# Hybrid Mamba-2 / latent-attention step: one mask tile, constant rows filled beside their tiles, an earlier table load; in the page stage a negated running maximum, two gather buffers and rotary keys read where they land

## The chip, the cores and the metric

The kernel runs on one core of a Trainium2 chip. The core has a matrix engine (TensorE, PE in the profile; its weight loads are listed as PEld), a vector engine (VectorE, DVE), an activation engine (ScalarE, ACT), a general engine (GpSimd, POOL) and a queue engine (SyncE, SP) that issues most DMA transfers. The metric is the device time of one launch in microseconds. The median of three runs of the kernel before is 1981.43 us (1976.2 to 1981.67).

## The reference, cut to what matters

Two layers work on a prompt (1 x 1024 tokens) and on a group of samples (8 sequences of 8 tokens, each with 2048 cached positions). Layer 0 is a Mamba-2 mixer, layer 1 is multi-head latent attention (MLA) with 16 heads; a norm follows. The change touches the attention of layer 1 only. All values are fp32.

```python
def latent_partial(q_lat, q_pe, ckv, kpe, mask):
    s = (jnp.einsum('bqhc,bkc->bhqk', q_lat, ckv)          # latent part, 256 wide
         + jnp.einsum('bqhr,bkr->bhqk', q_pe, kpe)) * MLA_SCALE   # rotary part, 32 wide
    if mask is not None:
        s = jnp.where(mask, s, NEG_INF)
    m = jnp.max(s, axis=-1)
    p = jnp.exp(s - m[..., None])
    return m, jnp.sum(p, axis=-1), jnp.einsum('bhqk,bkc->bhqc', p, ckv)

def merge_partial(pa, pb):
    m = jnp.maximum(ma, mb)
    ca, cb = jnp.exp(ma - m), jnp.exp(mb - m)
    return m, la * ca + lb * cb, aa * ca[..., None] + ab * cb[..., None]
# prompt: o = softmax(q k^T) v per head, causal, 1024 queries
# samples: latent_partial over the 8 new tokens, then one page of 128 positions after the other
#          (16 pages of the cache per sequence, picked by page_table), merged as above
# both: h = h + (o * silu(gate)) @ w_out ; y = rms_norm(h) * final_norm_w
```

## The kernel before, in words

Every fp32 product is made of three matmuls on rounded halves: a value x is split into `xh` (a cast to the matmul's rounded type fp32r) and `xl = x - xh`, and the product is `xh*wh + xl*wh + xh*wl`. ACT mostly makes the high halves, DVE or POOL the low ones.

The Mamba layer runs to about 1090 us, the projections of the MLA layer to about 1343 us. What the change touches comes after that.

**Prompt heads (`mla_heads`, about 1343 to 1712 us).** For each of 16 heads there are 12 blocks of 128 keys by up to 512 queries. `qk` makes scores `st` from `kTh/kTl` and `qTh/qTl`, ACT makes the exponential twice, once as a rounded high half `th` (L1341) and once as `P` (L1342), POOL or DVE the low half `tl = P - th` (L1344), and `pv` adds `th*Vh + th*Vl + tl*Vh` into `o` (L1361 to L1363). The tiles `qT` and `kT` have 98 rows: 96 of query or key and two constant rows (ones in `kTh`, zeros in `kTl` and `qTl`), which carry the negative row maximum into the matmul. The value tiles `V` have 64 columns of ones, which give the row sums. Between the blocks the program puts units of preparation: `maxpass` of the next head (`sc`, a reduction `mx` with the mask `mk`), `prep_kv` (keys `kp`, split into `kTh`, `kTl`), `prep_q` (`qs`, queries). Before the first block the tables of ACT are changed (a table load, L1390), and `Heads.open` fills the constant rows of four key tiles, of `qTl2` and of `V1` and loads the mask a second time, into a tile of its own.

**Pages of the sample group (`Sample.flow`).** 32 items, four for each sequence; an item is 512 cached positions. For one item: POOL gathers the rows `pgr` from the cache with an indirect DMA, ACT makes the high half `kvh` (L1632), POOL the low half `kvl` (L1633, one operation 1024 wide), PE transposes `pgr` into `ct` (L1622), ACT and DVE make `cTh`, `cTl`; seven matmuls make the scores `sc` (six latent ones and one with the rotary keys `tk`, which SP loads as `tkr` for two items and POOL rounds into `tk` for one, L1550). `softmax` then takes the maximum `mx` (L1567), the new running maximum `mn` (L1570), its negated scaled form `nm` (L1573), and ACT the exponential `P` (L1576) and the factor `f` for the old sums (L1580). PE transposes `P` into `pt` (L1660), ACT and DVE split it, and matmuls add to the output `o`; `ac` is the accumulator of a sequence. The first 11 steps of this flow lie between the blocks of heads 14 and 15; the others run with the output projection.

**Output projection (`MlaOut.pieces`).** Eight tiles of 128 prompt tokens: the heads' gated output `og` is loaded (0.5 MB), split into `oh` (ACT) and `ol` (DVE), multiplied with the halves `w5h`, `w5l` of the output weights (48 matmuls of 512 columns each for every half), added to the residual `h`, squared and summed (`sq`, `ss`), normed (L1877, `h<-h,ss,fw`) and stored. Its pieces are put between the items, one tile for every four items. The halves of the weights are made from `w5r`/`w5p` (L1808, L1809) when the heads have ended.

**What sets the order.** PE and POOL run in the order of the program, which is written by hand here (`step`, `turn`, `flow`, `merge`). ACT, DVE and the queue of SP are ordered by a scheduler with a model of the time of each operation, except for operations that the program pins with `keep_in_program_order`. Buffers come from pools; `bufs=1` means that a new tile of that tag waits until the last reader of the old one has ended. The tag `og5` is such a tag: the loaded `og` and the scratch tile `junk` of the squares share one buffer.

Of the kernel before, what the change touches and what calls it, by code (L numbers as in the profile page):

```python
# [16 lines left out]
D = 1024  # L17
# [51 lines left out]


def RT(nc):
    return nc.gpsimd.tensor_copy
# [1031 lines left out]
class Heads:  # L1104
    def __init__(self, k, st):
# [3 lines left out]
        self.wuv = I["mla_w_uv"][0].rearrange("c h n -> c (h n)")  # L1109
        vp = st.enter_context(open_pool(tc, name="vp3", bufs=1))  # L1110
# [3 lines left out]
        self.kT = [k.kT]  # L1114
        self.add_k(vp, 1)
        self.qT = []
# [3 lines left out]
    def start(self, st):  # L1120
        k, nc = self.k, self.k.nc
        self.sp = st.enter_context(open_pool(k.tc, name="q0", bufs=1))
        self.load_mask()
# [4 lines left out]
    def load_mask(self):  # L1128
        nc = self.k.nc
        mk = self.sp.tile([128, 640], F32, name="mk")  # L1130
# [31 lines left out]
    def open(self, st, psum):  # L1162
# [5 lines left out]
        for a, b in self.kT:  # L1168
            nc.gpsimd.memset(a[96:98].bitcast(F32), 1.0)
            nc.gpsimd.memset(b[96:98].bitcast(F32), 0.0)  # L1170
        self.add_q(sp, 2)
        self.add_v(sp, 1)
        self.load_mask()
# [12 lines left out]
    def prep_group(self, hg):  # L1186
# [10 lines left out]
        split(k, *wv, raw)  # L1197
        yield
# [18 lines left out]
    def prep_kv(self, h):  # L1217
# [171 lines left out]
def mla_heads(k, hd, sm, early, st):  # L1389
    k.tc.keep_in_program_order(k.nc.scalar.preload_act_table_set("natural_log_exp_and_others"))  # L1390
# [84 lines left out]
class Sample:  # L1475
# [65 lines left out]
    def load_tk(self, n):  # L1541
        k, nc = self.k, self.k.nc
        self.tkr = self.ep.tile([96, 4, 256], F32, tag="tkr", name=f"tkr{n}", bufs=1)
        for j in range(3):
            src = k.kpe_d[j % 2][:, :, 128 * n : 128 * n + 256].rearrange("r c x -> c r x")
            nc.sync.dma_start(self.tkr[32 * j : 32 * j + 32], src)

    def round_tk(self, n):
        tk = self.ep.tile([96, 4, 128], F32R, tag="tk", name=f"tk{n}", bufs=2)
        RT(self.k.nc)(tk, self.tkr[:, :, 128 * (n % 2) : 128 * (n % 2) + 128])  # L1550
        self.tk[n] = tk
# [12 lines left out]
    def softmax(self, name, s, n, m_old):  # L1564
# [3 lines left out]
        if m_old is not None:  # L1568
            m = self.small(name, "mn4", 1)
            nc.vector.tensor_scalar(m, mx, m_old, None, op0=ALU.max)  # L1570
            mx = m
        nm = self.small(name, "nm4", 1)
# [413 lines left out]
```

## Time and profile before

| | |
|---|---|
| median of the runs (three) | 1981.43 us (1976.2 to 1981.67) |
| the profiled execution: its time, its span | 1988.45 us, 1986.7 us |
| PE busy | 1909.0 us (96% of the span), 12001 matmuls |
| DVE, ACT, POOL busy | 1204.0 us (61%), 1110.3 us (56%), 837.9 us (42%) |
| mean granted TensorE clock | 0.988 of full speed |
| moved by DMA | 202.12 MB, mean 102 GB/s |

The span is the time from the first to the last instruction of the profiled execution. "Busy" leaves out register, branch and DMA-issuing instructions. In rows of groups the columns are the line, the engine, the operation, output and inputs with their shapes, the count, then the busy time, the mean of one in ns, and the idle time before the group with the work that ended it. In rows of the timeline they are start (us), duration (us), engine, line, operation, output and inputs, and in brackets the idle time of the engine just before, with what ended it.

### The profile page before, as it was taken

How to read it: one execution, taken by the hardware profiler on the slowest of the kernel's cores; microseconds unless marked ns; L12 is line 12 of the kernel's file. 1: busy time of each engine (PE TensorE's matmuls, PEld its weight loads, DVE VectorE, ACT ScalarE, POOL GpSimd, SP SyncE). 2: the span in 40 equal slices, each digit the busy share in tenths (PEclk: the TensorE clock that was granted, in tenths of full speed). 3: DMA queues.
4: the chain of work that ended last, by engine and by line, in shares of the span. 5: the costliest groups of instructions: out<-in, count | busy, mean ns of one | idle time of the engine just before them, and what ended most of it. 6: DMA issues, size and time to landing. Idle time of an engine off the chain costs nothing. (4 is left out here: it accounts for less than half of the span.)

```text
span 1986.7 us, 33396 instructions
## 1 busy us (share of the span) xinstructions
PE 1909.0 (96%) x12001; PEld 1738.7 (88%) x12001; DVE 1204.0 (61%) x2439; ACT 1110.3 (56%) x2535; POOL 837.9 (42%) x1018
## 2 busy tenths in 40 slices
PE   6999999999999999899999999998999999899998
PEld 5999999999999999788787998997888887688887
DVE  4557575756665656755434114566788787766665
ACT  5456666666666666633214224436777777645552
POOL 1537455555655555443003221204333335755541
PEclk9999999999999999999999999999999999899999
DMA  4223323332333332645433242222111113544441
GB/s 152 59 65 88 90 84 96 83 106 83 95 83 95 81 96 89 200 153 183 148 126 121 89 165 66 99 84 74 45 50 40 50 40 100 189 139 140 138 146 38
DMA packets 181228, 202.12 MB, mean 102 GB/s; under 512 B 18844, under 2 KB 147752, under 8 KB 180680
## 3 DMA queue, kind: packets, MB, share of 16 engines
q1 hardware_dynamic: 176008, 180.21, 29.9%
q0 software_dynamic: 4976, 19.66, 3.1%
q8 instruction: 95, 1.56, 0.3%
q14 instruction: 69, 0.57, 0.1%
q10 hardware_dynamic: 80, 0.13, 0.0%
HBM read 146.65 MB, written 53.28 MB: 101 GB/s over the span
## 5 line engine op out<-in xcount | busy, mean ns | idle before, releaser
L88 PE MATMUL pj<-xh,wih 128*128 128x384 f32 (+1 forms) x768 | 255.8, 337 | 5.0 <-ACT xh L250 4.4
L88 PE MATMUL pj<-xl,wih 128*128 128x384 f32 (+1 forms) x768 | 255.3, 332 | 0.6 <-DVE xl L251 0.6
L88 PE MATMUL pj<-xh,wil 128*128 128x384 f32 (+1 forms) x768 | 254.6, 332 | 0.0
L1344 POOL TENSOR_TENSOR tl<-P,th 128x384 fp32r<-128x384 f32 (+1 forms) x96 | 91.9, 957 | 160.8 <-ACT P L1342 119.2
L487 DVE SCALAR_TENSOR_TENSOR acc<-raw,vec,acc 128x1112 f32<-128x1112 f32 x96 | 141.6, 1476 | 25.8 <-ACT acc L483 24.9
L88 PEld LDWEIGHTS pj<-xh,wih 128*128 128x128 f32 x768 | 145.1, 190 | 6.8 <-ACT xh L250 5.1
L88 PEld LDWEIGHTS pj<-xl,wih 128*128 128x128 f32 x768 | 145.7, 190 | 1.9 <-DVE xl L251 0.9
L88 PEld LDWEIGHTS pj<-xh,wil 128*128 128x128 f32 x768 | 145.5, 189 | 0.4
L100 PE MATMUL pz<-wih,xh 128*128 128x256 f32 x504 | 142.8, 287 | 0.8 <-ACT z L528 0.8
L100 PE MATMUL pz<-wil,xh 128*128 128x256 f32 (+1 forms) x504 | 140.2, 284 | 0.0
L1341 ACT ACTIVATE th<-st 128x512 fp32r<-128x512 f32 x192 | 94.5, 492 | 75.7 <-PE st L1337 54.9
L591 ACT ACTIVATE M<-M,tok 128x128 f32<-128x128 f32 (+1 forms) x288 | 90.9, 386 | 68.6 <-DVE M L588 68.4
L100 PE MATMUL pz<-wih,xl 128*128 128x256 f32 x448 | 128.3, 286 | 0.0
L1633 POOL TENSOR_TENSOR kvl<-pgr,kvh 128x1024 fp32r<-128x1024 f32 x32 | 77.6, 2424 | 71.6 <-ACT kvh L1632 71.6
L100 PEld LDWEIGHTS pz<-wih,xh 128*128 128x128 f32 x504 | 96.0, 190 | 1.6 <-ACT z L528 1.2
L588 DVE TENSOR_TENSOR M<-M,negu 128x512 f32<-128x512 f32 x64 | 52.2, 815 | 69.0 <-DMA M<-acs_d 68.7
L1342 ACT ACTIVATE P<-st 128x512 f32<-128x512 f32 x192 | 93.4, 486 | 0.0
L100 PEld LDWEIGHTS pz<-wil,xh 128*128 128x128 f32 (+1 forms) x504 | 92.7, 184 | 0.7
L130 DVE TENSOR_TENSOR wil<-wraw,wih 128x512 fp32r<-128x512 f32 x88 | 71.2, 815 | 30.4 <-ACT wih L129 27.1
L1344 DVE TENSOR_TENSOR tl<-P,th 128x512 fp32r<-128x512 f32 x96 | 74.8, 779 | 21.8 <-ACT P L1342 21.3
L574 POOL TENSOR_TENSOR xdd<-xsT,tok 128x256 f32<-128x256 f32 x64 | 51.2, 800 | 81.3 <-ACT xsT L560 81.0
L100 PEld LDWEIGHTS pz<-wih,xl 128*128 128x128 f32 x448 | 85.3, 190 | 0.1
(827 smaller groups left out, 6343.5 us busy)
## 6 DMA issues: line engine op xcount, KB each, us to landing
wraw<-in_ssd_w_in SPq DMA_DIRECT2D x92, 256.0 KB
M<-acs_d SPq DMA_DIRECT2D x64, 256.0 KB
s<-in_state_ssm SPq DMA_DIRECT2D x32, 256.0 KB
y_d<-y SPq DMA_DIRECT2D x64, 128.0 KB
out_s_ssm<-s SPq DMA_DIRECT2D x32, 256.0 KB
wraw<-in_ssd_w_out SPq DMA_DIRECT2D x12, 512.0 KB
q_d<-qt SPq DMA_DIRECT2D x32, 192.0 KB
qp<-q_d SPq DMA_DIRECT2D x8, 768.0 KB
```

The costliest lines, as they stand in the source:

```text
L88: nc.tensor.matmul(out, a, b, start=(i == 0), stop=(i == n - 1))
L100: nc.tensor.matmul(o, a, b, start=(j == 0), stop=(j == len(ops) - 1))
L130: (eng or nc.vector).tensor_tensor(lo, src, hi.bitcast(F32), op=ALU.subtract)
L487: last = nc.vector.scalar_tensor_tensor(acc, raw[:, j : j + n], k.convw[j][:, blk : blk + 1], acc, op0=ALU.mult, op1=ALU.add)
L574: nc.gpsimd.tensor_tensor(v3(xdd), v3(xsT), hb(2), op=ALU.mult)
L588: nc.vector.tensor_tensor(M[:m, :, :m], M[:m, :, :m], (k.negs if smp else k.negu)[:m, :m].unsqueeze(1).to_broadcast([m, 4, m]), op=ALU.add)
L591: nc.scalar.activation(M[:m, h, :m], M[:m, h, :m], AF.Exp, bias=tk[:, 0, 4 * g + h : 4 * g + h + 1])
L1341: nc.scalar.activation(th[:, :n], ps[:, :n], AF.Exp, scale=SCALE)
L1342: nc.scalar.activation(P[:, :n], ps[:, :n], AF.Exp, scale=SCALE)
L1344: eng.tensor_tensor(tl[:, :n], P[:, :n], th[:, :n].bitcast(F32), op=ALU.subtract)
L1633: nc.gpsimd.tensor_tensor(rl, raw, rh.bitcast(F32), op=ALU.subtract)
```

## The change

1. The mask is loaded once, into a tile of the pool `qp` that lasts for the layer. The second load and its memset of 384 columns (L1131) are gone.
2. The constant rows of a key tile are filled when the tile gets its content (`ones_rows`): those of tiles 0 and 1 in `__init__`, those of 2 and 3 behind their rotary casts in `prep_kv`. The constant rows of `qTl2` are filled in `prep_q` of head 2, the ones columns of `V1` in `prep_group` of the second group of heads.
3. The table load of ACT stands in the loop of the query projection, 3 of its copies before the end, where it stood at the start of the heads.
4. `softmax` keeps `nm`, the negated and scaled running maximum, as its state: one operation takes the place of `mn` and `nm`, and `f` is the exponential of `nm - old`.
5. The rotary keys land in a tile of the rounded type and are read from there, the half of an item with a stride (4 runs of 128 columns, 256 apart); the round casts on POOL (32) are gone. All seven score matmuls now name their operands in three dimensions.
6. In `halves`, the cast `kvh` is kept in program order, and `kvl` is made by two operations of 512 columns.
7. `og5` has two buffers, and `junk` a tag of its own (`sq5`).

```diff
@@ Heads
+        self.load_mask()
         vp = st.enter_context(open_pool(tc, name="vp3", bufs=1))
...
         self.kT = [k.kT]
+        self.ones_rows(0)
         self.add_k(vp, 1)
+        self.ones_rows(1)
...
     def load_mask(self):
         nc = self.k.nc
-        mk = self.sp.tile([128, 640], F32, name="mk")
+        mk = self.k.qp.tile([128, 640], F32, name="mk")
...
     def add_q(self, pool, j):
-        self.k.nc.gpsimd.memset(t[1][96:98].bitcast(F32), 0.0)
+        if j < 2:
+            self.k.nc.gpsimd.memset(t[1][96:98].bitcast(F32), 0.0)
...
     def add_v(self, pool, j):
-        nc.gpsimd.memset(t[0][:, :, :, 64:128].bitcast(F32), 1.0)
-        nc.gpsimd.memset(t[1][:, :, :, 64:128].bitcast(F32), 0.0)
         self.V.append(t)
+        if j == 0:
+            self.ones_cols(0)
+
+    def ones_cols(self, j):
+        for t, x in zip(self.V[j], (1.0, 0.0)):
+            self.k.nc.gpsimd.memset(t[:, :, :, 64:128].bitcast(F32), x)
...
@@ Heads.open
-        for a, b in self.kT:
-            nc.gpsimd.memset(a[96:98].bitcast(F32), 1.0)
-            nc.gpsimd.memset(b[96:98].bitcast(F32), 0.0)
         self.add_q(sp, 2)
         self.add_v(sp, 1)
-        self.load_mask()
+
+    def ones_rows(self, j):
+        nc, (a, b) = self.k.nc, self.kT[j]
+        nc.gpsimd.memset(a[96:98].bitcast(F32), 1.0)
+        nc.gpsimd.memset(b[96:98].bitcast(F32), 0.0)
...
@@ Heads.prep_group
         split(k, *wv, raw)
+        if hg == 1:
+            self.ones_cols(1)
@@ Heads.prep_kv
             if pr == 1:
-                self.rope_keys(2)
-                self.rope_keys(3)
+                for x in (2, 3):
+                    self.rope_keys(x)
+                    self.ones_rows(x)
@@ Heads.prep_q
+        if h == 2:
+            nc.gpsimd.memset(self.qT[2][1][96:98].bitcast(F32), 0.0)
@@ mla_heads
-    k.tc.keep_in_program_order(k.nc.scalar.preload_act_table_set("natural_log_exp_and_others"))
@@ Sample.load_tk
-        self.tkr = self.ep.tile([96, 4, 256], F32, tag="tkr", name=f"tkr{n}", bufs=1)
+        tk = self.ep.tile([96, 4, 256], F32R, tag="tk", name=f"tk{n}", bufs=2)
         for j in range(3):
             src = k.kpe_d[j % 2][:, :, 128 * n : 128 * n + 256].rearrange("r c x -> c r x")
-            nc.sync.dma_start(self.tkr[32 * j : 32 * j + 32], src)
-
-    def round_tk(self, n):
-        tk = self.ep.tile([96, 4, 128], F32R, tag="tk", name=f"tk{n}", bufs=2)
-        RT(self.k.nc)(tk, self.tkr[:, :, 128 * (n % 2) : 128 * (n % 2) + 128])
-        self.tk[n] = tk
+            nc.sync.dma_start(tk[32 * j : 32 * j + 32].bitcast(F32), src)
+        for j in range(2):
+            self.tk[n + j] = tk[:, :, 128 * j : 128 * j + 128]
@@ Sample.softmax
-    def softmax(self, name, s, n, m_old):
+    def softmax(self, name, s, n, old):
         nc.vector.reduce_max(mx, s, axis=AX.X)
-        if m_old is not None:
-            m = self.small(name, "mn4", 1)
-            nc.vector.tensor_scalar(m, mx, m_old, None, op0=ALU.max)
-            mx = m
-        nm = self.small(name, "nm4", 1)
-        nc.vector.tensor_scalar(nm, mx, -SCALE, None, op0=ALU.mult)
+        nm = self.small(name, "nm4", 1, 4)
+        if old is None:
+            nc.vector.tensor_scalar(nm, mx, -SCALE, None, op0=ALU.mult)
+        else:
+            nc.vector.tensor_scalar(nm, mx, -SCALE, old, op0=ALU.mult, op1=ALU.min)
...
-            nc.scalar.activation(f, m_old, AF.Exp, bias=nm, scale=SCALE)
-        return mx, P, l, f
+            nc.scalar.activation(f, old, AF.Exp, bias=nm, scale=-1.0)
+        return nm, P, l, f
@@ Sample.halves
-        nc.scalar.copy(rh, raw)
-        nc.gpsimd.tensor_tensor(rl, raw, rh.bitcast(F32), op=ALU.subtract)
+        k.tc.keep_in_program_order(nc.scalar.copy(rh, raw))
+        for j in (0, 2):
+            nc.gpsimd.tensor_tensor(rl[:, j : j + 2], raw[:, j : j + 2], rh[:, j : j + 2].bitcast(F32), op=ALU.subtract)
@@ MlaOut.pieces
-                g = sp.tile([128, 8, 128], F32, tag="og5", name=f"og5{i}", bufs=1)
+                g = sp.tile([128, 8, 128], F32, tag="og5", name=f"og5{i}", bufs=2)
...
-            junk = sp.tile([128, D], F32, tag="og5", name=f"sq5{i}", bufs=1)[:m]
+            junk = sp.tile([128, D], F32, tag="sq5", name=f"sq5{i}", bufs=1)[:m]
@@ mla_q's loop
         for n, _ in enumerate(mla_q(k, mid)):
+            if n == 32:
+                tc.keep_in_program_order(nc.scalar.preload_act_table_set("natural_log_exp_and_others"))
```

The order of PE's instructions is the same in both kernels; the other engines' orders move at three places.

POOL where the heads begin, before: the memsets of the constant rows and columns and of the mask, then the first low half `tl` (384 wide), then the four rotary casts (`kTh`, `kTl` of key tiles 2 and 3) and the next low half.

```order
L1170 MEMSET kTl_15386 2x1024
L1137 MEMSET qTl_15396 2x1024
L1146 MEMSET Vh_15398 128x16x64
L1147 MEMSET Vl_15399 128x16x64
L1131 MEMSET mk 128x384
L1344 TENSOR_TENSOR tl<-P,th 128x384
L1160 CAST kTh_15383<-kTh_13121 32x1024
L1160 CAST kTl_15384<-kTl_13122 32x1024
L1160 CAST kTh_15385<-kTh_13121 32x1024
L1160 CAST kTl_15386<-kTl_13122 32x1024
```

The same place after: the first `tl` comes first, and the memsets of key tiles 2 and 3 stand among the casts.

```order
L1354 TENSOR_TENSOR tl<-P,th 128x384
L1163 CAST kTh_15388<-kTh_13121 32x1024
L1163 CAST kTl_15389<-kTl_13122 32x1024
L1176 MEMSET kTh_15388 2x1024
L1177 MEMSET kTl_15389 2x1024
L1163 CAST kTh_15390<-kTh_13121 32x1024
L1163 CAST kTl_15391<-kTl_13122 32x1024
L1176 MEMSET kTh_15390 2x1024
L1177 MEMSET kTl_15391 2x1024
L1354 TENSOR_TENSOR tl<-P,th 128x128
```

The memsets of `qTl2`, `V1` and the mask have left this place, and those of key tiles 2 and 3 have moved behind the first `tl`, ahead of the second.

ACT in the blocks of head 14, before: the exponentials `th`, `P` of the blocks and among them the casts `kvh` of the first two items.

```order
L1342 ACTIVATE P<-st_1_2_19755 128x512
L1374 ACTIVATE rl_0_19749<-rl_0_19749 64x512
L1632 CAST kvh<-pgr_19697 128x1024
L1341 ACTIVATE th<-st_1_3_19777 128x512
L1342 ACTIVATE P<-st_1_3_19777 128x512
L1632 CAST kvh<-pgr_19705 128x1024
L1341 ACTIVATE th<-st_1_4_19797 128x512
L1342 ACTIVATE P<-st_1_4_19797 128x512
L1341 ACTIVATE th<-st_1_5_19817 128x384
L1342 ACTIVATE P<-st_1_5_19817 128x384
```

The same place after:

```order
L1352 ACTIVATE P<-st_1_2_19752 128x512
L1384 ACTIVATE rl_0_19746<-rl_0_19746 64x512
L1351 ACTIVATE th<-st_1_3_19774 128x512
L1352 ACTIVATE P<-st_1_3_19774 128x512
L1351 ACTIVATE th<-st_1_4_19794 128x512
L1352 ACTIVATE P<-st_1_4_19794 128x512
```

And where the first `kvh` stands now, 18 operations further on, behind the exponential `P40n` of the first sequence's own tokens, between the first four and the last eight blocks of head 15:

```order
L1351 ACTIVATE th<-st_0_3_19957 128x128
L1352 ACTIVATE P<-st_0_3_19957 128x128
L1581 ACTIVATE P40n,l40n<-sn_19976,nm40n 128x8
L1637 CAST kvh<-pgr_19694 128x1024
L1351 ACTIVATE th<-st_1_0_19991 128x512
L1352 ACTIVATE P<-st_1_0_19991 128x512
```

The casts of the first two items have moved behind the blocks that they stood among.

DVE once in four items, where a tile of the output projection ends (`h`, `ss`) and the next one's `ol` is made, before:

```order
L1851 TENSOR_TENSOR h_21333<-h_21333,p_21523 128x512
L1681 SCALAR_TENSOR_TENSOR ac_21356<-ac_21356,f_21511,o_21647 128x256
L1868 TENSOR_TENSOR ss_21339<-ss_21339 128x1
L1869 TENSOR_SCALAR ss_21339<-ss_21339 128x1
L1877 SCALAR_TENSOR_TENSOR h_21333<-h_21333,ss_21339,fw 128x512 x2
L130 TENSOR_TENSOR cTl_0_21671<-ct_0_21665,cTh_0_21670 128x512
L130 TENSOR_TENSOR pTl_21680<-pt_21674,pTh_21679 128x512
L130 TENSOR_TENSOR cTl_1_21689<-ct_1_21683,cTh_1_21688 128x512
L1567 TENSOR_REDUCE mx_21700<-sc_21692 128x1
L130 TENSOR_TENSOR ol_21728<-og_21729,oh_21727 128x1024
L1570 TENSOR_SCALAR mn_21702<-mx_21700,mx44n 128x1
L1573 TENSOR_SCALAR nm_21704<-mn_21702 128x1
```

The same place after:

```order
L1855 TENSOR_TENSOR h_21289<-h_21289,p_21473 128x512
L126 TENSOR_TENSOR ol_21672<-og_21673,oh_21671 128x1024
L1687 SCALAR_TENSOR_TENSOR ac_21312<-ac_21312,f_21463,o_21594 128x256
L1872 TENSOR_TENSOR ss_21295<-ss_21295 128x1
L1873 TENSOR_SCALAR ss_21295<-ss_21295 128x1
L126 TENSOR_TENSOR cTl_0_21619<-ct_0_21613,cTh_0_21618 128x512
L1881 SCALAR_TENSOR_TENSOR h_21289<-h_21289,ss_21295,fw 128x512 x2
L126 TENSOR_TENSOR pTl_21628<-pt_21622,pTh_21627 128x512
L126 TENSOR_TENSOR cTl_1_21637<-ct_1_21631,cTh_1_21636 128x512
L1573 TENSOR_REDUCE mx_21648<-sc_21640 128x1
L1578 TENSOR_SCALAR nm_21650<-mx_21648,nm44n 128x1
```

The low half `ol` of the next tile has moved from between the reduction `mx` and `nm` to the start of the piece, `cTl` ahead of the norm of `h`, and `mn` is gone.

More of the change, by code (lines that the diff above doesn't have):

```diff
@@ L68 @@
 FLOW = 11
-def RT(nc):
-    return nc.gpsimd.tensor_copy
 def WQ(nc):
@@ L1577, in softmax @@
         f = None
-        if m_old is not None:
+        if old is not None:
             f = self.small(name, "f4", 1)
-            nc.scalar.activation(f, m_old, AF.Exp, bias=nm, scale=SCALE)
-        return mx, P, l, f
+            nc.scalar.activation(f, old, AF.Exp, bias=nm, scale=-1.0)
+        return nm, P, l, f
     def first_scores(self, b):
@@ L1628, in halves @@
     def halves(self, n):
-        nc, sp = self.k.nc, self.sp
+        k, nc = self.k, self.k.nc
         raw = self.raw.pop(n)
         rh, rl = (x[:, n % 2].rearrange("p (r c) -> p r c", r=4) for x in (self.k.kvh, self.k.kvl))
-        nc.scalar.copy(rh, raw)
-        nc.gpsimd.tensor_tensor(rl, raw, rh.bitcast(F32), op=ALU.subtract)
+        k.tc.keep_in_program_order(nc.scalar.copy(rh, raw))
+        for j in (0, 2):
+            nc.gpsimd.tensor_tensor(rl[:, j : j + 2], raw[:, j : j + 2], rh[:, j : j + 2].bitcast(F32), op=ALU.subtract)
         self.hl[n] = (rh, rl)
@@ L1640, in scores @@
         c0, c1 = self.cT.pop((n, 0)), self.cT.pop((n, 1))
-        mm3(nc, ps, [
+        mm3(nc, ps.rearrange("p (r c) -> p r c", r=4), [(x, y if len(y.shape) == 3 else y.rearrange("p (r c) -> p r c", r=4)) for x, y in (
             (k.qlh[:, 0, b], c0[0]), (k.qlh[:, 0, b], c0[1]), (k.qll[:, 0, b], c0[0]),
             (k.qlh[:, 1, b], c1[0]), (k.qlh[:, 1, b], c1[1]), (k.qll[:, 1, b], c1[0]),
-            (k.qpr[:, b], self.tk.pop(n))])
+            (k.qpr[:, b], self.tk.pop(n)))])
         self.ps[n] = ps
@@ L1737, in flow @@
                 self.late_loads()
-            if t:
-                self.round_tk(n + 1)
             if n % 2 == 0 and n + 2 < N:
@@ L1897, in layer_mla @@
         mla_in(k, right, mid)
-        qp = st.enter_context(open_pool(tc, name="qp", bufs=1))
+        k.qp = qp = st.enter_context(open_pool(tc, name="qp", bufs=1))
         k.qlh = qp.tile([128, 2, NB, 128], F32R, name="qlh")
```

1 line of the change is left out of this document (removed).

## The prediction

> **What bounds the kernel now.** I read the page's first part first, then PE's waits in the three stretches that the change touches, then a table of windows for the clock. The first line shares out the busy time.
>
> ```profile
> PE 1909.0 (96%) x12001; PEld 1738.7 (88%) x12001; DVE 1204.0 (61%) x2439; ACT 1110.3 (56%) x2535; POOL 837.9 (42%) x1018
> ```
>
> PE is the bound; no other engine is near full over the span. The change leaves PE's instructions and their order alone, so a gain can come only from PE's idle time and from time at a lowered clock. PE's waits in 1340 to 1366 us (where the heads begin), 1660 to 1746 (end of the heads and hand-over to the output projection) and 1762 to 1937 (steady pages) are, with total, count and longest in us:
>
> ```profile
> PE sc L1298 <- DVE mx L1303: 2.7, 2, 1.4
> PE o L1363 <- POOL tl L1344: 2.1, 1, 2.1
> ...
> PE act L1691 <- DVE ac L1684: 4.4, 1, 4.4
> PE pt L1660 <- ACT P L1576: 2.9, 3, 1.4
> PE o L88 <- DVE pTl L130: 2.0, 1, 2.0
> PE st L1330 <- ACT P L1342: 1.6, 1, 1.6
> PE o40n L1612 <- ACT pn L1605: 1.2, 1, 1.2
> ...
> PE pt L1660 <- ACT P L1576: 7.8, 6, 1.3
> ```
>
> That is 4.8, 12.1 and 7.8 us. Windows of the same execution, with window, length, busy time of PE, PEld, DVE, ACT, POOL, then PE's clock, DMA share and GB/s:
>
> ```profile
> 1359.00:1366.00 7.00, 6.42 (x19) 5.17 (x20) 3.21 (x8) 3.94 (x8) 3.13 (x4) 0.52 0.17 41
> 1672.00:1680.00 8.00, 7.13 (x25) 6.46 (x26) 2.31 (x7) 3.69 (x10) 3.37 (x4) 0.57 0.09 10
> 1680.00:1690.00 10.00, 10.00 (x68) 8.93 (x66) 7.09 (x9) 9.04 (x22) 6.99 (x7) 1.00 0.38 125
> 1693.00:1700.00 7.00, 6.84 (x20) 5.36 (x21) 3.82 (x6) 2.89 (x8) 6.65 (x5) 0.53 0.40 118
> 1720.00:1728.00 8.00, 6.77 (x28) 5.83 (x29) 6.66 (x14) 6.61 (x12) 6.89 (x5) 0.57 1.05 273
> 1736.00:1746.00 10.00, 5.86 (x18) 4.77 (x19) 8.83 (x8) 3.33 (x5) 6.41 (x4) 0.66 0.69 215
> 1762.00:1937.00 175.00, 166.97 (x1002) 143.45 (x1001) 118.12 (x245) 93.48 (x201) 91.07 (x69) 1.00 0.47 144
> ```
>
> Five periods have about half the clock. Length times (1 - clock) gives 3.4, 3.4, 3.3, 3.4 and 3.4 us lost, each behind one of the waits above. So such a wait costs its length and some 3.4 us more. The six waits of the steady pages draw no drop: clock 1.00.
>
> **The change part by part.** *Entry of the heads (mask, constant rows, table).* Rows in order of time, and one group (busy, mean ns of one, idle):
>
> ```profile
> 1344.22 1.28 ACT L1390 ACT_TABLE_LOAD   x1
> 1346.86 0.51 ACT L1342 ACTIVATE P<-st 128x384 f32<-128x384 f32 x1
> 1348.33 0.95 POOL L1169 MEMSET kTh<- 2x1024 f32 x1 [83.91 <-DMA mk<-in_c_maskn]
> 1353.30 0.99 POOL L1344 TENSOR_TENSOR tl<-P,th 128x384 fp32r<-128x384 f32 x1
> 1353.91 0.50 PE L1298 MATMUL sc<-kTh,qTh 96*128 96x512 f32 x1 [1.35 <-DVE mx L1303]
> 1358.43 2.34 POOL L1344 TENSOR_TENSOR tl<-P,th 128x128 fp32r<-128x128 f32 x2
> 1359.58 0.47 PE L1363 MATMUL o<-tl,Vh 128*128 128x128 f32 x1 [2.10 <-POOL tl L1344]
> ...
> L1160 POOL CAST kTl<-kTl 32x1024 fp32r<-32x1024 f32 x2 | 2.1, 1036 | 0.0
> ```
>
> POOL is the late engine: it makes memsets from 1348.3 to the `tl` of 1353.3, while `P` has been ready since 1347.37. Afterwards the table load (1.28) no longer stands ahead of the exponentials, so `P` ends near 1346.1, `tl` at 1347.1. Behind it come four casts of 1.04 and four memsets of 0.95: 8.0, to 1355.1. The next `tl` takes half of the pair's 2.34, so it ends near 1356.3; PE now restarts at 1359.58, so that is -3.3. PE would be there by 1357.48 (the start of its 2.10 wait) less the mask's 1.35 and up to the first 1.4, at 1354.7: a wait near 1.5 stays, as long as those that drew a drop, so I leave the 3.4 in. Bounds: -1.4 (the mask's wait alone) to -6.7 (3.3 and the drop).
>
> *Three memsets moved into the heads* (`qTl2`, two of `V1`): a memset takes 0.95; POOL has 3.9 of 7 us free in 1359 to 1366, yet `tl` waits behind it if it comes at a bad moment. +0.5, between 0 and 2.9 (three in full).
>
> *Casts of the first two items.*
>
> ```profile
> 1670.78 1.05 ACT L1632 CAST kvh<-pgr 128x1024 fp32r<-128x1024 f32 x1 [1.44 <-DMA pgr<-in_cache_ckv,ptidx]
> 1672.87 0.53 PE L1330 MATMUL st<-qTh,kTh 98*128 98x256 f32 x1 [1.60 <-ACT P L1342]
> ```
>
> The second cast (the first stands a block earlier) waits 1.44 for its gather and runs 1.05 with exponentials of head 14 queued behind it, and PE stands for 1.60, then runs through the drop of 1672 to 1680. With the casts behind head 14 the wait and its 3.4 go: -5.0. The first cast now comes behind `P40n`, where ACT has 9.04 of 10 us taken: its 1.05 is late there, and `pn` is what is late next (1.2 now): +1.0. Net -4.0; bounds 0 (the wait and its drop come back there) and -5.0.
>
> *Hand-over.*
>
> ```profile
> 1712.54 1.04 ACT L1632 CAST kvh<-pgr 128x1024 fp32r<-128x1024 f32 x1 [1.93 <-POOL og L1375]
> 1722.30 1.05 ACT L1808 CAST w5h<-w5r 128x1024 fp32r<-128x1024 f32 x1 [0.38 <-DMA w5r<-in_mla_w_out]
> ```
>
> The exponential `P` for which PE waits up to 1.4 (`pt`) comes right behind this cast, and will stand ahead of it: -1.04. The second buffer lets SP issue the second tile's `og` load right behind the first transfers, ahead of the second set of `w5r`. Its 0.52 MB at the 273 GB/s of the window 1720 to 1728 are +1.9 for casts that wait for DMA already. Net +0.7 (0.9, less 0.2 since one of these casts waits only 0.38); bounds -4.5 (one wait and its drop) to +5.3 (1.9 and a new drop). The 4.4 us behind `ac` (POOL's low halves run beside it) I leave.
>
> *Costed at nothing:* the 32 round casts, `kvl` in halves, `mn`.
>
> ```profile
> L1550 POOL CAST tk<-tkr x32: 602/626/1063, 1685.8 to 1944.5; 96x512 fp32r<-96x512 f32 x32
> L1633 POOL TENSOR_TENSOR kvl<-pgr,kvh x32: 2358/2395/3371, 1686.4 to 1949.3; 128x1024 fp32r<-128x1024 f32 x32
> ```
>
> POOL is busy 91 of 175 us in the steady window, so 32 x 0.63 = 20 us off it, and two halves of 1.27 (between the 384-wide `tl`'s 0.99 and this row's 2.40 for 1024, in a straight line) for one 2.40, 32 x 0.14 = +4.5 on it, lie beside PE. Without that cover they would be -0.6 and +0.14 an item. `tk` has two buffers for two items each; its load has an item's time more than the one `tkr` had.
>
> *Steady pages.* Once in four items (rows of the fifth of six):
>
> ```profile
> 1829.02 3.55 DVE L1877 SCALAR_TENSOR_TENSOR h<-h,ss,fw 128x512 f32<-128x512 f32 x2 [0.69 <-POOL ss L1870]
> 1834.89 1.21 DVE L130 TENSOR_TENSOR ol<-og,oh 128x1024 fp32r<-128x1024 f32 x1
> 1836.02 0.20 DVE L1570 TENSOR_SCALAR mn<-mx,mx44n 128x1 f32<-128x1 f32 x1
> 1836.26 0.15 DVE L1573 TENSOR_SCALAR nm<-mn 128x1 f32<-128x1 f32 x1
> 1836.51 0.69 ACT L1576 ACTIVATE P<-sc,nm 128x512 f32<-128x512 f32 x1 [2.09 <-DVE nm L1573]
> 1837.34 0.66 PE L1660 MATMUL pt<-ident,P 128*128 128x128 f32 x4 [1.28 <-ACT P L1576]
> ```
>
> DVE is late: the norm of `h`, three low halves, the reduction, then `ol` ahead of `mn` and `nm`. Afterwards `ol` (1.13 from its start to `mn`'s) stands ahead of that stretch, in front of `ac`, and `mn` (0.24) is gone: `nm` comes 1.37 sooner on paper. Some of `ol` stays in the way, since DVE idles only 0.69 before `h`, less than `ol` takes: I leave 0.3 of each wait. 6 x (1.28 - 0.3) = -5.9; bounds -4.0 (`ol` half in the way) and -7.7.
>
> Sum: -3.3 + 0.5 - 4.0 + 0.7 + 0 - 5.9 = -12.0, against the profiled execution's 1988.45, so 1976.4. That execution lies 7.0 above the median of the runs, 1981.43; on that basis the forecast is 1969.4.
>
> [...] The score matmuls read the rotary keys with a stride now. The nearest rows are a matmul whose moving operand is eight runs of 16, and one with contiguous operands, both 128x128:
>
> ```profile
> L1701 PE MATMUL lo<-accT,wv x32: 274/275/276, 1965.4 to 1968.9; 128*128 128x128 f32 x32
> L1622 PE MATMUL ct<-ident,pgr x256: 270/272/421, 1680.3 to 1942.0; 128*128 128x128 f32 x128
> ```
>
> 275 against 272 ns: the runs cost nothing that shows, so the sum has nothing for it. [...]
>
> The waits of 1.2 to 2.1 us above stood ahead of periods of half clock. [...]
>
> **The rivals.**
> First, the forecast, 1962 to 1975.5: chance 0.50.
> Second, deeper: the waits shorten enough that more drops vanish: -6.7 at the entry, 0, -5.0, -4.5, 0, -7.7 = -23.9, 1957.5. For it: each wait is near the smallest that drew a drop (1.2). Against: it needs all places at once. Its band is 1956 to 1962: 0.17.
> Third, hidden or put elsewhere: waits come back one place later. Entry -1.4, casts -1.0, hand-over +5.3, pages -5.9 = -3.0, 1978.4. For it: the clock drops wherever one wait of 1.2 stays, ACT is full behind `P40n`, and the hand-over moves 273 GB/s. Against: the steady gain depends on none of these. Band 1975.5 to 1987.4: 0.21.
> Fourth, slower: the score matmuls slow down. They are 32 x 7 = 224, of 512 columns; one such follows another by 0.24 us (rows 1355.81 and 1356.05 here).
>
> ```profile
> 1355.81 0.40 PE L1330 MATMUL st<-qTh,kTh 98*128 98x512 f32 x1
> 1356.05 0.39 PE L1331 MATMUL st<-qTl,kTh 98*128 98x512 f32 x1
> ```
>
> At half rate, 224 x 0.24 = +54, 2023; from 18/224 = 0.08 us each on it ends above the bound of "same". If only the 32 strided ones halve, 32 x 0.24 = 7.7, 1977, the third's band. Against it stand the rows above. 0.12, with what I overlook.
>
> **How the numbers follow.** I predict the first case's sum, 1969.4. A measurement of this kernel can tell about 0.3% (6 us) from no change: faster is below 1975.5, slower above 1987.4. Faster is the first two cases, 0.67; same the third, 0.21; slower the fourth, 0.12. The first two hold 0.67; up to 1984 the third adds some 0.14 more, and 1984 also takes in the worst ends summed (-1.4 + 2.9 + 0 + 5.3 - 4.0 = +2.8, 1984.2). The range is 1956 to 1984.
>
> **What would show it.** Right: the first `tl` near 1347 and PE's wait for it 1.5 or less; no wait for the mask at 1352; no wait for `P` of head 14 and full clock in 1672 to 1680; six waits of `pt` summing to 2 us or less; `sc<-tk,qpr` with the other score matmuls' duration; POOL without `tk` casts. Wrong: a new wait behind `pn` near 1692 with half clock, a longer wait for `w5h` near 1720, a wait for `kvl` in the pages, score matmuls well above 0.40 us.

## The result, and the profile after

The changed kernel takes 1968.92 us in the median of seven runs (1966.84 to 1973.42); the kernel before takes 1978.86 in the median of seven (1976.2 to 1981.67; the three of them shown earlier had 1981.43). The ratio is 0.9948, 95% interval 0.9935 to 0.9961: about 10 us faster, where 12.0 were forecast. The profiled execution of the changed kernel took 1968.92 us, its span 1967.1.

The first part of its page:

```profile
PE 1902.0 (97%) x12001; PEld 1732.5 (88%) x12001; DVE 1188.6 (60%) x2407; ACT 1109.2 (56%) x2535; POOL 822.2 (42%) x1017
```

PE's waits in it: the entry of the heads (1340 to 1366 us), heads 14 and 15 (1640 to 1700), the hand-over (1700 to 1750) and the pages (1750 to 1925).

```profile
PE o L1373 <- POOL tl L1354: 2.5, 1, 2.5
...
PE st L1340 <- DMA qTh<-nd: 2.4, 1, 2.4
PE o40n L1617 <- ACT pn L1610: 1.4, 1, 1.4
...
PE p L96 <- DVE ol L126: 4.8, 1, 4.8
PE o L84 <- DVE pTl L126: 1.7, 1, 1.7
...
PE act L1697 <- ACT kvh L1637: 1.6, 6, 0.3
```

At the entry one wait is left of four. In the pages the six waits of 1.3 before `pt` are gone, and six of 0.3 before another operation (`act`, which waits for the cast `kvh`) stand there now. Two waits are new: 2.4 for `qTh`, which comes from memory, and 4.8 for `ol` at the hand-over, where 4.4 for `ac` stood before.

PE executes the same instructions in the same order in both kernels, so the start of each can be compared. The profile of before that the prediction worked on is 19.5 us longer than this one, twice the difference of the medians; a second profile of the unchanged kernel (1981.88 us, first experiment) is nearer its median, and the table uses it.

| stretch (time in the changed kernel) | predicted | measured against the second profile of before |
|---|---|---|
| up to the heads (1340) | 0 | -0.8 |
| entry of the heads, with the moved memsets (to 1366) | -3.3 + 0.5 | -4.6 |
| heads 1 to 13 (to 1650) | 0 | +0.2 |
| heads 14 and 15 (to 1700) | -4.0 | +1.0 |
| hand-over (to 1745) | +0.7 | -2.6 |
| pages to the end | -5.9 | -6.2 |
| sum | -12.0 | -13.0 |

The sum is that of these two executions; single executions of one kernel lie 5 to 7 us apart, and the medians differ by 9.9.

### The profile page after: what moved, and what is told of

The parts are those of the page before. It is cut to its first block, busy times and chain, and to the rows that moved or that the text cites. A ratio compares the mean times of both kernels' runs of the same rounds, so it can differ in the third digit from the quotient of the medians.

```text
span 1967.1 us, 33409 instructions
## 1 busy us (share of the span) xinstructions
PE 1902.0 (97%) x12001; PEld 1732.5 (88%) x12001; DVE 1188.6 (60%) x2407; ACT 1109.2 (56%) x2535; POOL 822.2 (42%) x1017
## 5 line engine op out<-in xcount | busy, mean ns | idle before, releaser
L1639 POOL TENSOR_TENSOR kvl<-pgr,kvh 128x512 fp32r<-128x512 f32 x64 | 85.3, 1350 | 74.3 <-ACT kvh L1637 74.3
L1354 DVE TENSOR_TENSOR tl<-P,th 128x512 fp32r<-128x512 f32 x96 | 69.2, 721 | 21.9 <-ACT P L1352 21.5
```

The source lines that it names most:

```text
L1354: eng.tensor_tensor(tl[:, :n], P[:, :n], th[:, :n].bitcast(F32), op=ALU.subtract)
L1639: nc.gpsimd.tensor_tensor(rl[:, j : j + 2], raw[:, j : j + 2], rh[:, j : j + 2].bitcast(F32), op=ALU.subtract)
```

## The experiments

Each edit starts from the changed kernel, unless it says otherwise. Ratios are to the kernel before on the same chip, with their 95% intervals. Differences in microseconds to the changed kernel are between medians of separate measurements, partly on other chips; the kernel before had medians of 1978.3 to 1978.9 in all of them.

**The kernel before once more.** No edit.

> The kernel before, unchanged, profiled once more. The profiled execution of the kernel before took 1988.45 us while its other executions took 1976 to 1982; between the two profiles the difference is 19.5 us, between the medians 9.9. Theory A: the waits of PE are the same in every execution, but how much of the time behind a wait is granted at half clock differs from one execution to the next. Then this profile has the same waits within 0.2 us (1.35 for the mask, 2.1 for tl, 1.6 in head 14, 4.4 for ac, six of 1.3 in the pages), a time of 1976 to 1983, and fewer low-clock stretches after 1343 us: 5 to 12 us of them instead of 17. Theory B: some wait was longer in that one execution; then waits differ by 5 us or more in sum.

It took 1981.88 us. PE's waits in heads 14 and 15 (1640 to 1700 us) of this profile:

```profile
PE st L1330 <- ACT P L1342: 1.4, 2, 1.0
PE o40n L1612 <- ACT pn L1605: 1.2, 1, 1.2
```

Two windows of 16 us around these waits, first of this profile, then of the first profile of before (columns as in the prediction, the clock is third from the end):

```profile
1664.00:1680.00 16.00, 14.83 (x88) 12.31 (x87) 10.29 (x25) 12.60 (x28) 10.18 (x10) 1.00 0.45 125
1684.00:1700.00 16.00, 14.49 (x73) 11.79 (x72) 12.61 (x17) 9.46 (x25) 10.00 (x8) 0.89 0.23 66
```

```profile
1664.00:1680.00 16.00, 13.75 (x54) 10.97 (x54) 8.87 (x19) 9.24 (x18) 8.36 (x9) 0.79 0.35 88
1688.00:1704.00 16.00, 14.49 (x58) 11.20 (x58) 11.52 (x14) 9.17 (x21) 9.98 (x8) 0.79 0.25 66
```

16 us times (1 - clock) is the time lost: 0 and 1.8 here, 3.4 and 3.4 there. Between the two profiles 6.7 us are lost from 1500 to 1715 us; 5.0 of them are this low clock, the rest is a shorter wait for `P` (0.99 for 1.60) and shorter waits for constant rows of `qTh` from memory. The waits elsewhere agree within 0.2. Theory A holds but for these waits: the time lost to low clock from 1343 to 1950 us fell from 17.1 to 12.0 us, the upper end of what it said.

**Second rotary load later.**

```diff
-            nc.sync.dma_start(tk[32 * j : 32 * j + 32].bitcast(F32), src)
+            (k.tc.keep_in_program_order if n == 2 else id)(nc.sync.dma_start(tk[32 * j : 32 * j + 32].bitcast(F32), src))
```

> The changed kernel, with the loads of the second pair's rotary keys (three transfers of 128 KB) kept in the order of the program, so that they stand behind the constant rows of head 15 in SP's queue instead of ahead of those of head 14. Theory A: the new wait of PE for qTh in the changed kernel (2.37 us at 1656.8, with a low clock behind it) comes from these three transfers. Then the wait is below 0.3 us and the time falls by 2.4 to 5 us against the changed kernel, to a ratio of about 0.993 to before. Theory B: the wait comes from the 0.5 MB of output weights that stand in the queue there in both kernels; then it stays at 2 us or more and the time is that of the changed kernel (0.9948) within 1 us.

First the place in the changed kernel: SP's queue, and the matmul that waits.

```profile
1651.36 0.43 SPq L1555 DMA_DIRECT2D tk<-kpe_dh  x1
1651.82 0.44 SPq L1555 DMA_DIRECT2D tk<-kpe_dl  x1
1652.30 0.43 SPq L1555 DMA_DIRECT2D tk<-kpe_dh  x1
1653.14 0.24 SPq L1328 DMA_DIRECT2D qTh<-nd  x1
...
1656.76 0.47 PE L1340 MATMUL st<-qTh,kTh 98*128 98x512 f32 x1 [2.37 <-DMA qTh<-nd]
```

With two buffers the second pair's keys can be loaded at once, and the scheduler put the three transfers (128 KB each) ahead of the 4 KB of constant rows that head 14 needs. With the edit no wait for `qTh` is left between 1640 and 1700, one of 0.8 for `tl` is new, and PE gains 2.0 us there: theory A as to the place. Time 1967.64 us, ratio 0.9943 (0.9924 to 0.9961). That is not told apart from the changed kernel's 0.9948, and less than the 2.4 to 5 us that theory A gave; in the trace 1.0 us is lost again at the hand-over and 1.0 at the entry, where the low clock lasted longer in this execution.

**One buffer for `og`.**

```diff
-                g = sp.tile([128, 8, 128], F32, tag="og5", name=f"og5{i}", bufs=2)
+                g = sp.tile([128, 8, 128], F32, tag="og5", name=f"og5{i}", bufs=1)
-            junk = sp.tile([128, D], F32, tag="sq5", name=f"sq5{i}", bufs=1)[:m]
+            junk = sp.tile([128, D], F32, tag="og5", name=f"sq5{i}", bufs=1)[:m]
```

> The changed kernel with one buffer for og, shared with the scratch tile of the squares, as before; all else as changed. Theory A (the prediction's): the early ol ended the six waits of the pages. Then they come back with about 1.0 us each (the removed mn keeps 0.24 of 1.28), +5 to +6.5, and the hand-over loses the second og load, -1 to -4: +2 to +5 us against the changed kernel, ratio about 0.9965. Theory B: the shorter chain from the reduction to nm ended them; then the waits stay below 0.3 us and the time is no longer than that of the changed kernel, ratio 0.993 to 0.995.

PE's waits in the pages:

```profile
PE pt L1666 <- ACT P L1581: 6.2, 6, 1.1
```

Time 1974.79 us, ratio 0.9978 (0.9965 to 0.999): 5.9 us above the changed kernel. The interval does not overlap the changed kernel's (0.9935 to 0.9961). The waits are back with 1.0 each, as theory A said; the hand-over became 3.2 us longer in the trace, where it was to be shorter. A wait of 1.4 for `ac` is new there, and up to 1.7 us of the 3.2 are low clock.

**`og`'s buffers alone, on the kernel before.** The same two lines, the other way round.

> The kernel before with two buffers for og and a tag of its own for the scratch tile, nothing else. Theory A: the early ol is what ends the six waits of the pages. They fall from 1.28 to at most 0.5 us each (0.24 for mn that is still there, and rest), which is -5 to -6, and the second og load at the hand-over gives 0 to +3: ratio 0.997 to 0.999. Theory B: mn, or POOL's round casts that remain, keep a wait of 0.8 us or more in each; then the ratio is 0.999 or above.

```profile
PE pt L1660 <- ACT P L1576: 1.8, 6, 0.6
PE act L1691 <- DVE ac L1684: 1.1, 6, 0.2
```

The waits fall from 7.8 to 2.9 us in sum, theory A. The time is 1975.24 us, ratio 0.999 (0.9977 to 1.0003): at the edge between the theories, and by the time alone not told apart from no gain.

**The running maximum in two operations.**

```diff
-            nc.vector.tensor_scalar(nm, mx, -SCALE, old, op0=ALU.mult, op1=ALU.min)
+            nc.vector.tensor_scalar(m, mx, m_old, None, op0=ALU.max)
+        nm = self.small(name, "nm4", 1)
+        nc.vector.tensor_scalar(nm, m, -SCALE, None, op0=ALU.mult)
```

> The changed kernel with the two operations mn and nm of the running maximum again (32 more of 0.2 us on DVE); all else as changed. Theory A: in the pages DVE and ACT have some 0.2 us of slack once in four items (the wait that is left is 0.27, for kvh); then 0.2 more in front of the exponential costs 0 to 0.3 us in each of six places, 0 to +2 in all, ratio 0.995 to 0.996. Theory B: the negated maximum, not og's buffer, carries the gain in the pages (with og's buffer alone the period of four items fell from 32.02 to 31.5, in the changed kernel to 31.03); then 0.5 us a period come back, +3 us, and the ratio is 0.9965.

```profile
PE pt L1667 <- ACT P L1582: 1.1, 6, 0.2
PE act L1698 <- DVE ac L1691: 1.1, 6, 0.2
```

Time 1969.89 us, ratio 0.9951 (0.9938 to 0.9965): theory A. The start of the transposes `act`, which come once in four items, gives the period in the pages of each kernel. Two starts before, then two in the changed kernel:

```profile
1774.21 0.38 PE L1691 MATMUL act<-ident,ac 128*128 128x128 f32 x2
1806.24 0.38 PE L1691 MATMUL act<-ident,ac 128*128 128x128 f32 x2
```

```profile
1760.12 0.41 PE L1697 MATMUL act<-ident,ac 128*128 128x128 f32 x2 [0.27 <-ACT kvh L1637]
1791.16 0.41 PE L1697 MATMUL act<-ident,ac 128*128 128x128 f32 x2 [0.27 <-ACT kvh L1637]
```

On average the period is 32.02 us before, 31.35 with `og`'s buffers alone, 31.65 in the changed kernel with one buffer, 31.25 with the maximum in two operations, 31.03 in the changed kernel. So the buffer is worth about 0.6 to 0.7 of the 0.99, and the negated maximum 0.22; some 0.1 is left for the other parts.

**The casts `kvh` not pinned.**

```diff
-        k.tc.keep_in_program_order(nc.scalar.copy(rh, raw))
+        nc.scalar.copy(rh, raw)
```

> The changed kernel without the pin on the casts kvh; all else as changed. ACT then has the casts of the first two items among the exponentials of head 14 again. Theory A (the prediction's): these casts make the wait of PE for P in head 14 (1.6 us) and the half clock behind it. Then a wait of 1 us or more stands there again, the wait behind pn (1.4) becomes shorter, and the time is 2 to 5 us above the changed kernel, ratio about 0.9965. Theory B: the wait in head 14 only took the place of the wait for qTh, which is served by the same DMA queue; then head 14 loses nothing, and the time is that of the changed kernel within 1 us.

The waits in heads 14 and 15:

```profile
PE st L1340 <- DMA qTh<-nd: 2.5, 1, 2.5
PE o40n L1617 <- ACT pn L1610: 1.2, 1, 1.2
PE o L1373 <- POOL tl L1354: 1.0, 1, 1.0
```

No wait for `P` came back, though the casts stood among the exponentials again: PE is held 2.5 us by `qTh` just ahead. Head 14 lost 0.3 us in the trace (to 1680), which is theory B. Up to 1700 the balance says less: a wait of 1.0 for `tl` came in, and the 1.7 us of low clock that the changed kernel's profile has behind `pn` are absent. The time, 1971.24 us, ratio 0.9966 (0.9951 to 0.998), is 2.3 above the changed kernel with intervals that overlap; the trace has 1.4 more at the hand-over.

What the pin is worth without the wait for `qTh` was not measured by an edit of its own. The profiles give a hint. Eight of them have at most 0.6 us of waiting for `qTh` in head 14. In the four with the casts free (the two of before, the entry alone, `og`'s buffers alone) PE's longest wait for `P` there is 0.8 to 1.6 us; in the four with the casts pinned (rotary keys later, both edits, rows later, rotary keys as before) it is 0.3 at most, but waits for `tl` sum to 0.2 to 1.2 us, where the others have up to 0.5. These kernels differ in other parts too.

**The entry alone, on the kernel before** (parts 1 to 3 of the change).

```diff
+        self.ones_rows(0)
...
+        self.ones_rows(1)
...
-        for a, b in self.kT:
-            nc.gpsimd.memset(a[96:98].bitcast(F32), 1.0)
-            nc.gpsimd.memset(b[96:98].bitcast(F32), 0.0)
...
-        self.load_mask()
```

> The kernel before with the parts on the entry of the heads alone (one mask tile, constant rows beside their tiles, table load sooner). Theory A: the entry's gain stands by itself. Between the last query projection and 30 us later PE gains 4 to 5 us (4.5 in the changed kernel; the prediction had 2.8), the waits for the mask (1.35) and for mx (1.4) are gone, one wait for tl of about 2.5 stays with low clock behind it, and the time is 3 to 5 us below before, ratio 0.9975 to 0.9985. Theory B: part of the changed kernel's gain there comes from other parts or from chance in the low clock; then PE gains under 3 us there and the ratio is 0.999 to 1.

PE gains 3.5 us between 1340 and 1366, the waits for `mx` are gone, one of 2.4 for `tl` stays. A wait of 1.35 for `tk` at the hand-over is new. In the trace that lies between the theories (4 to 5, under 3); of the 4.6 of the changed kernel some 1.1 to 1.3 us were a shorter stretch of low clock. Time 1976.47 us, ratio 0.9992 (0.9983 to 1.0001): less than theory A's 3 to 5 us, and not told apart from no gain.

**The rotary keys as before.**

```diff
-        tk = self.ep.tile([96, 4, 256], F32R, tag="tk", name=f"tk{n}", bufs=2)
+        self.tkr = self.ep.tile([96, 4, 256], F32, tag="tkr", name=f"tkr{n}", bufs=1)
...
+        RT(self.k.nc)(tk, self.tkr[:, :, 128 * (n % 2) : 128 * (n % 2) + 128])
...
-        mm3(nc, ps.rearrange("p (r c) -> p r c", r=4), [...
+        mm3(nc, ps, [
```

> The changed kernel with the rotary keys as before: one buffer, rounded by POOL item by item (32 casts of 0.63 us), all score operands contiguous. Theory A: strided and three-dimensional operands cost PE nothing, and the second pair's load goes back behind the heads. Then the score matmuls take the same 0.39 to 0.40 us, the wait of 2.4 for qTh in head 14 is gone (-2 to -4), and a wait of 1.3 for tk at the hand-over comes in, as in the two kernels with the old tk: time within 2 us of the changed kernel. Theory B: the strides slow the matmuls; then the score matmuls become shorter by 0.02 us or more each (224 of them, 4.5 us) and the time falls by 4 us or more.

The rotary score matmuls from 1750 to 1915 us (minimum, median, maximum in ns), of the changed kernel and then of this one:

```profile
L84 PE MATMUL sc<-tk,qpr x21: 389/392/396, 1752.8 to 1908.0; 96*128 96x512 f32 x21
```

```profile
L88 PE MATMUL sc<-tk,qpr x21: 391/394/402, 1755.5 to 1910.9; 96*128 96x512 f32 x21
```

PE's longest wait at this one's hand-over (1700 to 1750):

```profile
PE sc L88 <- POOL tk L1563: 7.7, 1, 7.7
```

392 ns with the stride, 394 without: the operands cost nothing. The wait for `qTh` fell to 0.6 (theory A), but the wait for `tk` at the hand-over is 7.7, not 1.3. It is a wait for the load: POOL's cast stands ready 1.5 us before the keys arrive, and SP had issued them at 1706 to 1709 us, behind loads of the output weights.

```profile
1717.70 0.75 POOL L1563 CAST tk<-tkr 96x512 fp32r<-96x512 f32 x1 [1.53 <-DMA tkr<-kpe_dh]
```

Time 1972.72 us, ratio 0.9966 (0.9952 to 0.998), 3.8 above the changed kernel, beyond theory A's 2; the intervals overlap.

**`kvl` whole.**

```diff
-        for j in (0, 2):
-            nc.gpsimd.tensor_tensor(rl[:, j : j + 2], raw[:, j : j + 2], rh[:, j : j + 2].bitcast(F32), op=ALU.subtract)
+        nc.gpsimd.tensor_tensor(rl, raw, rh.bitcast(F32), op=ALU.subtract)
```

> The changed kernel with kvl made by one operation of 1024 columns. Theory A (the prediction's): the halving is hidden, since POOL is busy 81 of 165 us in the pages and DVE has slack; same time within 1 us, no new wait above 0.3 us in the pages. Theory B: with halves DVE's long operations get in between them (they wait while a POOL subtraction runs); then the norm of h takes longer than the 3.2 us it has now, and waits of 0.3 to 1 us come back in the pages, +2 to +5 us.

Time 1969.18 us, ratio 0.9958 (0.9944 to 0.9971), the waits in the pages 0.27 as in the changed kernel, the period 31.07: theory A. The norms of `h` spread more (minimum, median, maximum in ns), changed kernel first:

```profile
L1881 DVE SCALAR_TENSOR_TENSOR h<-h,ss,fw x8: 1490/1639/1782, 1783.6 to 1878.1; 128x512 f32<-128x512 f32 x8
```

```profile
L1880 DVE SCALAR_TENSOR_TENSOR h<-h,ss,fw x8: 737/1712/2699, 1780.3 to 1876.1; 128x512 f32<-128x512 f32 x8
```

The sum of two is the same within 0.2 us.

**Fifth low half of the output weights on DVE.**

```diff
-WENG = (2, 0, 2, 0, 2, 0, 2, 0)
+WENG = (2, 0, 2, 0, 0, 0, 2, 0)
```

> The changed kernel with the low half of the fifth output-weight tile made by DVE where POOL made it. In the changed kernel PE waits 4.8 us for the first tile's ol at the hand-over; DVE's ol takes 5.65 us there beside two POOL operations back to back (w5l 2.4, kvl 2.5), and 1.21 elsewhere. Theory A: DVE's ol is held up by POOL's operations. Then ol takes 1.2 to 3.7 us, the wait falls from 4.8 to 1 to 3, and the time falls by 2 to 5 us against the changed kernel, ratio about 0.993. Theory B: ol is held up by something else (its own inputs, the DMA traffic of 330 GB/s); then ol stays above 5 us and the time rises by the 1.2 us of DVE.

The place in the changed kernel, in order of time:

```profile
1714.31 2.39 POOL L1813 TENSOR_TENSOR w5l<-w5r,w5h 128x1024 fp32r<-128x1024 f32 x1
1714.57 5.65 DVE L126 TENSOR_TENSOR ol<-og,oh 128x1024 fp32r<-128x1024 f32 x1 [0.43 <-ACT oh L125]
1716.64 2.48 POOL L1639 TENSOR_TENSOR kvl<-pgr,kvh 128x512 fp32r<-128x512 f32 x2
1720.27 0.79 PE L96 MATMUL p<-w5h,ol 128*128 128x512 f32 x1 [4.81 <-DVE ol L126]
```

And with the edit:

```profile
1717.71 1.22 DVE L126 TENSOR_TENSOR ol<-og,oh 128x1024 fp32r<-128x1024 f32 x1
1718.98 0.51 PE L96 MATMUL p<-w5h,ol 128*128 128x512 f32 x1 [0.98 <-DVE ol L126]
...
1727.91 0.78 PE L1666 MATMUL pt<-ident,P 128*128 128x128 f32 x4 [2.97 <-ACT P L1581]
```

POOL's next operation now starts 0.4 us behind `ol`, and takes 3.23 us in place of 2.48:

```profile
1718.10 3.23 POOL L1639 TENSOR_TENSOR kvl<-pgr,kvh 128x512 fp32r<-128x512 f32 x2 [1.31 <-ACT kvh L1637]
```

So `ol` takes 1.22 us where it starts 0.4 us ahead, and POOL is held up in its place: theory A as to the cause. In the changed kernel `ol` ends at 1720.22, 1.1 us behind POOL's last subtraction, as if it had run only then. The wait for `ac` in the kernel before was of the same kind: an operation of 0.35 us elsewhere took 4.49 beside two subtractions of POOL.

```profile
1735.51 4.49 DVE L1684 TENSOR_SCALAR ac<-ac,ln 128x256 f32<-128x256 f32 x1
1735.16 2.37 POOL L1809 TENSOR_TENSOR w5l<-w5r,w5h 128x1024 fp32r<-128x1024 f32 x1
1737.47 2.36 POOL L1633 TENSOR_TENSOR kvl<-pgr,kvh 128x1024 fp32r<-128x1024 f32 x1
```

The time did not fall, 1969.88 us, ratio 0.9961 (0.9947 to 0.9976): a wait of 2.97 for `P` stands behind it, and the waits from 1700 to 1750 still sum to 7.5 us (7.7 in the changed kernel).

**Both edits.**

> The changed kernel with both edits: the second pair's rotary keys in the order of the program, and the fifth low half on DVE. Theory A: both waits (2.4 for qTh, 4.8 for ol) have the causes named, and the edits add up: 4 to 8 us below the changed kernel, ratio 0.991 to 0.993. Theory B: at the hand-over the waits only trade places (with the rotary keys alone they summed to 7.5 us as in the changed kernel, on other instructions); then the ratio is 0.993 to 0.995.

Time 1965.95 us, ratio 0.9944 (0.9929 to 0.9958). By the ratio it is theory B, not told apart from the changed kernel's 0.9948. In the trace the waits from 1700 to 1750 sum to 5.5 us, and PE gains 4.0 us on the changed kernel from 1340 to 1745, so part of the gain is kept there.

**Both edits, and the constant rows of key tiles 2 and 3 later.**

```diff
                 for x in (2, 3):
                     self.rope_keys(x)
-                    self.ones_rows(x)
...
+        if h in (2, 3):
+            self.ones_rows(h)
```

> The changed kernel with the two edits on the rotary keys and on the low half, and the constant rows of key tiles 2 and 3 filled one and some units later, behind the low halves of the first blocks instead of ahead of the second one. Theory A: these four memsets (3.8 us) make the wait of 2.5 us for tl that is left at the entry. Then the wait is gone or below 0.6 us, with it the low clock there (1.7 to 3.4 us), and PE is 3 to 6 us earlier at the end of the first head than with the two edits alone: ratio 0.990 to 0.993. Theory B: the casts of the rotary rows, or ACT, hold PE up there as well; then a wait of 1.5 us or more stays and the gain is at most 1.5.

POOL's second `tl` in the timeline (at 1355.12 in the changed kernel, whose profile is 1.3 us ahead of this one where the heads begin, so 3.7 us sooner):

```profile
1352.74 0.47 POOL L1355 TENSOR_TENSOR tl<-P,th 128x128 fp32r<-128x128 f32 x1
```

The only wait of PE above 0.3 us from 1340 to 1366:

```profile
PE st L1341 <- ACT P L1353: 0.9, 1, 0.9
```

And the window from 1352 to 1368 us, of this kernel, of the kernel before and of the changed kernel:

```profile
1352.00:1368.00 16.00, 14.77 (x82) 11.70 (x81) 13.07 (x29) 10.89 (x25) 9.38 (x10) 1.00 0.10 22
```

```profile
1352.00:1368.00 16.00, 12.55 (x50) 9.72 (x49) 9.90 (x24) 8.49 (x17) 11.18 (x12) 0.79 0.09 20
```

```profile
1352.00:1368.00 16.00, 13.49 (x67) 11.12 (x67) 11.77 (x25) 10.20 (x23) 9.68 (x11) 0.89 0.08 18
```

The wait for `tl` is gone and the clock stays full. Time 1963.46 us (1961.36 to 1964.5), ratio 0.9921 (0.9908 to 0.9934): theory A. Against the changed kernel's 0.9935 to 0.9961 the intervals just fail to overlap, so this version is faster than the kernel before and, barely clear of the noise, than the changed kernel; against the two edits alone (0.9929 to 0.9958) they overlap, so the part of the rows alone rests on the trace. From the start of the heads to 1366 PE gains 2.5 us on the changed kernel and on the two edits alone, a little less than theory A's 3: a wait of 0.9 for `P` has come in.

## Why the prediction was right, and where it was wrong

The time forecast, 1969.4, is nearly the one measured, 1968.92, but not by its own terms: that the two meet within 0.5 us is luck. Three terms were off and cancelled, and the seven runs of before lie 2.6 us below the three from which it started, so the gain is 9.9 us, not 12.0.

- *Pages, -5.9: right*, in size and cause. The period fell by 0.99 us, six times -5.9. `ol` ahead of the norm carries two thirds, `mn` 0.22 of it. The 0.3 that was to be left of each wait, because some of `ol` stays in the way, is 0.27 for another reason: PE waits for `kvh`, before `act`.
- *Entry, -3.3: right for the wait.* The matmul that waits for the second `tl` starts 3.3 us earlier. The wait that remains is 2.46, not 1.5, since PE arrives earlier than forecast. The other 1.3 us of the -4.6 is low clock, 1.7 us of it in place of 3.4. That is chance: of thirteen profiles with a wait of 1.9 to 2.6 us for this `tl` eight lost 3.4 us behind it and five lost 1.7.
- *Casts of the first two items, -4.0: wrong*, in two ways. The 5.0 that they were to free held 3.4 us of low clock that the second profile of before does not have, and there the wait was 0.99. And the part on `tk` said only that its load has more time; that an earlier load stands ahead of others in SP's queue was not followed. It cost PE 2.4 us and 1.7 us of low clock in head 14. The +1.0 at `pn` was 0.2 (1.38 for 1.19).
- *Hand-over, +0.7: wrong sign.* It is 2.6 us shorter. The wait for `ac`, which the prediction left alone, is gone, and one of 4.8 for `ol` stands in its place: both are an operation of DVE held up beside subtractions of POOL, in the kernel before `ac` (4.49 us where 0.35 is usual), in the changed one `ol` (5.65 us for 1.22). What became shorter are the waits for `P` (2.7 to 0.4 us in sum, where -1.04 was forecast) and the low clock between 1700 and 1750, 5.1 us lost in place of 6.8. With one `og` buffer the stretch is longer, not shorter; the second `og` load, the +1.9 of the sum, cost nothing that shows.
- *Costed at nothing* (casts of `tk`, halves of `kvl`, operands): right in the pages. The periods differ by 0.06 us or less. Not so at the hand-over, where PE waited 7.7 us for the old single buffer of `tk` in one kernel.
- *The fourth case*, slower score matmuls, is excluded: 392 ns with the stride against 394 without. That a strided operand could slow the matmuls was a supposition of the author's, against which the rows of before stood (275 against 272 ns). No run shows the half rate from which its 2023 and 1977 are worked out.

## What to carry to other kernels

When a second buffer lets a load go earlier, look at what stands behind it in the queue: three 128 KB transfers ahead of 4 KB cost a wait of 2.4 us, where PE of the kernel before had not waited for the load at all. A gain at such a place should be checked in the trace as well as in the time: here several waits only moved to the next instruction. A stretch of low clock behind a wait should be priced as a chance over several executions (0, 1.7 or 3.4 us lost behind one wait here), not at the value that one profile shows. On an engine that runs in program order, put fills that are needed late behind the work that the bound engine waits for, not merely beside their tile: here a wait of 2.5 us for `tl` was gone with four memsets of 0.95 to 0.98 us moved behind that `tl`.

## What the runs showed of the hardware

Low clock came in portions. Behind one wait, 0, 1.7 or 3.4 us were lost by length times (1 - clock) (5.1 behind three longer waits, of 3.8, 4.7 and 7.7 us), so stretches of 3.4 or 6.8 us at half clock: between 1359 and 1365 us of the first profile of before the granted clock is 0.50. These figures are upper bounds, since some stretches begin before the wait has ended. Behind the same wait of 1.2 to 1.4 us for `pn` six of fourteen profiles lost nothing, seven 1.7 and one 3.4. The 24 waits of 1.0 to 1.3 us in the pages of four profiles, one in some 32 us, never drew any. Every profile with a wait of 1.9 to 2.6 us at the entry lost 1.7 or 3.4 us there. What decides how much low clock a wait draws was not tested.

A DVE subtraction of 1.2 us took 5.65 us where it started 0.26 us behind the first of two low halves that POOL made back to back (`w5l`, then `kvl` in two operations), and 1.22 where it started 0.4 us ahead of POOL's operation, which then took 3.23 us in place of 2.48. At this place the changed kernel and four of its variants show such an `ol` (4.8 to 5.95 us, each ending 1.1 us behind POOL's last subtraction), and the three profiles with the pages as before (the two of before, the entry alone) show an `ac` of 4.45 to 4.49 us, where 0.35 is usual.
